# Branch A's tensor-engine order written out by hand, with the convolution taps kept out of the inverses

## The chip, the cores and the metric

The kernel runs on one core of a Trainium2 chip. The metric is the device time of one execution in microseconds (us), and the median of several runs stands for a kernel. The engines are named as the profile names them: PE is the tensor engine (PEld its weight load), DVE the vector engine, ACT the scalar engine, POOL the GpSimd engine, and SP the queue that issues nearly all DMAs.

## What is computed

The reference is a trunk of two layers over 256 context tokens and 512 latent tokens of 1024 channels, in float32. Each layer normalises and modulates its input, projects it with one wide matrix, runs four branches, and merges them through gates and an output matrix. Branch A is the one that matters here, with branch B's convolution beside it:

```python
def wkv_scan(s0, w, kk, b, k, v, r, reverse):
    def step(s, inp):
        w_t, kk_t, b_t, k_t, v_t = inp[:5]
        sa = jnp.einsum('bhvk,bhk->bhv', s, kk_t)
        s = s * w_t[:, :, None, :] - sa[..., None] * b_t[:, :, None, :] + v_t[..., None] * k_t[:, :, None, :]
        o = None if r is None else jnp.einsum('bhvk,bhk->bhv', s, inp[5])
        return s, o
...
def conv_module(glu, conv_w, conv_b, ln_w, ln_b):
    u = glu[..., :CONV_CH] * jax.nn.sigmoid(glu[..., CONV_CH:])
    u = lax.conv_general_dilated(u, conv_w[:, None, :], window_strides=(1,),
...
```

Branch A (8 heads of 64) runs `wkv_scan` forwards and backwards over context and latent tokens, normalises each head's output and adds a bonus. Branch B is a depthwise convolution of 31 taps over 512 channels. Branches C (windowed attention) and D (latent attention) follow in the kernel after branch A and are not touched by the change.

## The kernel before

Every large projection is a `dense`: 8 tiles of 128 input channels, each as three float32r matmuls (`mm3`: high by high, high by low, low by high), over 256 context columns and 512 latent columns. The weights of one output tile of 128 channels come by DMA (`raw`), ACT rounds them (`wh`) and POOL subtracts (`wl`), in two halves; three buffers of `wh` and `wl` are shared by all. The sums stand in the PSUM tag `d`, two banks, until ACT or DVE has taken them out.

Branch A works on four pairs of heads (p = 0 to 3). The sequence of 768 tokens is cut into 12 chunks of 64, taken two at a time (c = 0, 2, ... 10). For each pair:

- `rwkv_prep` makes decays and keys of 256 tokens at a time (three groups g), with short matmuls into the one bank of tag `E`.
- `rwkv_gram` makes the chunks' Gram matrices (`G`).
- `rwkv_inverse` inverts 32x32 blocks of all 12 chunks at once: ACT copies (L707), a DVE transpose (L710), 31 steps of two dependent DVE instructions (L717, L719), and two DVE transposes (L721, L722). PE takes no part in it.
- `rwkv_factors` turns the inverse into the factors `TM` with small PE matmuls (L739, L748).
- `rwkv_chunk` runs the recurrence. Each of the 12 chunks is three links: z (L820, then DVE makes `Xc`, L822), u (L826, then ACT copies one half, L827, and DVE the other, L828), q (L833, then DVE makes the new state `M`, L841). A link needs the one before.
- `rwkv_post` normalises the outputs and stores them.

`side_units` lists projections that branch A does not need: the convolution's gated input (`glu`, two tiles each, four of them), ten tiles for branches C and D, sixteen gates `z`, and three (layer 0) or eight (layer 1) tiles of branch gates. `fill` emits them in groups, FILL = 3, 3, 5, 7, 10, before and after the pairs, and what is left after the last pair. Each `glu` unit also emits its `conv_taps`: 31 DVE instructions (L966) on 256 context columns (layer 0 only) and 31 on 512 latent columns, with the lowest priority.

The order on each engine is fixed before the run. A planner, the tile scheduler, walks the program with a model of the instructions' times and takes on each engine the ready instruction of the highest priority (program order, shifted by `high_priority`). Where `manual_schedule` is set for PE, PE keeps the program's order instead; before the change that holds inside a few short groups of matmuls only. At run time each engine goes through its list in order and waits at semaphores.

Of the kernel before, what the change touches and what calls it, by code (L numbers as in the profile page):

```python
# [2 lines left out]

# [15 lines left out]
D = 1024  # L19
# [194 lines left out]

class Net:
# [70 lines left out]
    def mm3(self, ps, wh, wl, xh, xl, first, last):  # L286
        mm = self.nc.tensor.matmul
        mm(ps, lhsT=wh, rhs=xh, start=first, stop=False)  # L288
        mm(ps, lhsT=wh, rhs=xl, start=False, stop=False)  # L289
        mm(ps, lhsT=wl, rhs=xh, start=False, stop=last)  # L290

    def dense(self, w, xs, segs, psum=None):

        outs = []
        nk = len(xs)
        for s0, s1 in segs:
            ps = (psum or self.pd)(s1 - s0)
            outs.append(ps)
            for h, (wh, wl) in enumerate(w):
                for i in range(4):  # L300
                    k, c = 4 * h + i, slice(128 * i, 128 * i + 128)
                    self.mm3(ps, wh[:, c], wl[:, c], xs[k][0][:, s0:s1], xs[k][1][:, s0:s1], k == 0, k == nk - 1)
        return outs

    def proj(self, l, name, segs):

        if (name, segs) in self.begun:
            return self.begun.pop((name, segs))
        return self.dense(self.split_w(self.a["w_in"][l, TILES[name]]), self.hx, segs)
# [153 lines left out]
    def rwkv(self, l, rp):  # L463
# [35 lines left out]

        def fill(n):  # L500
            for _ in range(min(n, len(units))):
                units.pop(0)()

# [10 lines left out]
        for g in range(NG):  # L514
            self.rwkv_prep(rp, g, wa, st)
        self.rwkv_gram(rp, st)
        self.rwkv_factors(st, *self.rwkv_inverse(rp, st))
        self.rwkv_proj(l, rp, 1)
        fill(FILL[0])
        for p in range(4):  # L520
            nxt = None
            if p < 3:
                nxt = self.rwkv_state(l, rp, p + 1)
                self.rwkv_prep(rp, 0, wa, nxt)
            for c in (0, 2, 4, 6):
                self.rwkv_chunk(rp, st, c)
            if nxt:
                for g in range(1, NG):
                    self.rwkv_prep(rp, g, wa, nxt)
            self.rwkv_chunk(rp, st, 8)  # L530
            if nxt:
                self.rwkv_gram(rp, nxt)
                diag = self.rwkv_inverse(rp, nxt)
            self.rwkv_chunk(rp, st, 10)
            if nxt:
                self.rwkv_factors(nxt, *diag)
            if p == 2:
                right.close()
                self.window_inputs(l)
            self.rwkv_post(rp, p, st)  # L540
            if p == 3:
                self.window_rope()
            if p < 2:
                self.rwkv_proj(l, rp, p + 2)
            fill(FILL[p + 1])
            st = nxt
        fill(len(units))

    def rwkv_proj(self, l, rp, p, names="kvr", segs=(SEG_C, SEG_X)):

        nc = self.nc
        for nm in names:
# [3 lines left out]
            for ps, (s0, s1) in zip(self.proj(l, f"{nm}{p}", sg), sg):  # L556
# [7 lines left out]
    def rwkv_state(self, l, rp, p):  # L564
        nc = self.nc
        st = {"p": p, "KB": {}, "KR": {}, "v2": {}, "M": None, "o": {}, "c": None}
# [13 lines left out]
    def rwkv_prep(self, rp, g, wa, st):  # L580

# [35 lines left out]
        nc.tensor.matmul(ps, lhsT=self.c("blk"), rhs=sq, start=True, stop=True)  # L617
        kk = T("kk", "kk", 1)
# [4 lines left out]
        for d in range(2):  # L623
# [4 lines left out]
            ps = self.pE([128, n])  # L628
            lora(ps, 1, d)
            th = T("th", "th", 1)  # L630
            S.activation(th, ps, AF.Tanh, bias=dcol("a0h", dc), scale=0.5)
# [6 lines left out]
            ps = self.pE([128, n])  # L638
            lora(ps, 0, d)
            lw = T("lw")  # L640
            S.activation(rv(lw), ps, AF.Tanh, bias=dcol("w0h", dc), scale=0.5)
# [17 lines left out]
        if readout:  # L659
# [3 lines left out]
            nc.tensor.matmul(ps, lhsT=self.c("blk"), rhs=kds[0], start=True, stop=True)  # L663
            bv = T("bv")
# [3 lines left out]
    def rwkv_gram(self, rp, st):  # L668

        nc = self.nc  # L670
        mask = self.c("mask")
        st["G"] = []
        for c in range(0, NCH, 2):
            x, cl = c // GC, c % GC
            KB, KR = st["KB"][x], st["KR"][x]
            w = 64 if (self.last and x == 0) else 128
            G = rp.tile([128, 2, 2, 2, 128], F32, tag="G", name=self.n("G"), bufs=NCH // 2 + 1)
            st["G"].append(G)
            pss = [self.pA([128, 2, 2, 128]) for j in range(2)]
            for i in range(2):  # L680
                for d in range(2):
                    for j in range(2):
                        rows = slice(64 * j, 64 * j + 64)
                        nc.tensor.matmul(pss[j][:, i, d, :w],  # L684
                                         lhsT=KB[rows, d, cl + i].rearrange("p a b -> p (a b)"),
                                         rhs=KR[rows, cl + i, 0:w // 64, d, :],
                                         start=True, stop=True)
            for j, ps in enumerate(pss):
                nc.vector.tensor_tensor(out=G[:, j, :, :, :w].rearrange("p i d w -> p (i d) w"),  # L689
                                        in0=ps[:, :, :, :w].rearrange("p i d w -> p (i d) w"),  # L690
                                        in1=mask[:, :w].unsqueeze(1).to_broadcast([128, 4, w]), op=ALU.mult)

    def rwkv_inverse(self, rp, st):
# [16 lines left out]
        V.transpose(out=flat(B), in_=flat(AT))  # L710
# [11 lines left out]
        V.transpose(out=U.rearrange("p q t -> p t q"), in_=X.rearrange("p s t -> p t s"))  # L722
        return U, TA

    def rwkv_factors(self, st, U, TA):
# [7 lines left out]
        pss = []  # L733
        for q0, q1 in ((0, 16), (16, 24)):
# [6 lines left out]
            for d in range(2):  # L741
                b = slice(64 * d + 32, 64 * d + 64)
                S.copy(Y[b, q0:q1, :], ps[b])
            ps = self.pA([128, q1 - q0, 32])
# [15 lines left out]

    def rwkv_chunk(self, rp, st, c):
        cur = st["c"] or self.chunk_front(rp, st, c)
        st["c"] = self.chunk_front(rp, st, c + 2) if c + 2 < NCH else None
        self.chunk_back(rp, st, c, *cur)

    def chunk_front(self, rp, st, c):
# [20 lines left out]
        for d in range(2):  # L787
            h = half[1 - d]
            V.tensor_copy(VU[h, d], psb[h, 0])
        for i in range(2):  # L790
# [7 lines left out]
    def chunk_back(self, rp, st, c, KBt, VU, X0):  # L798

        nc, tc = self.nc, self.tc  # L800
# [3 lines left out]
        KR, G, TM, Dl = st["KR"][g], st["G"][c // 2], self.TM, st["Dl"]  # L804
        T = lambda nm, shape, bufs=2: rp.tile(shape, F32, tag=nm, name=self.n(nm), bufs=bufs)
        read = not (self.last and g == 0)
        Ms = []
        for i in range(2):
# [6 lines left out]
            u, q = (bank[:, x, 64:192].rearrange("p (a b) -> p a b", a=2) for x in range(2))  # L815
            X = X0[:, i]
            if M is not None:
# [4 lines left out]
                V.tensor_tensor(out=X, in0=X0[:, i], in1=z, op=ALU.subtract)  # L822
            for j in range(2):
                for d in range(2):
                    h = half[d]
                    mm(u[h, j], lhsT=TM[h, 2 * c + 2 * j + i, :], rhs=X[h, j], start=True, stop=True)  # L826
            S.copy(VU[half[0], 0, i], u[half[0]])  # L827
            V.tensor_copy(VU[half[1], 1, i], u[half[1]])  # L828
            if c + i == NCH - 1:
                break  # L830
            for d in range(2):
                for j in range(2):
                    mm(q[half[j], d], lhsT=KBt[:, i, d, j], rhs=VU[:, d, i, j], start=True, stop=True)  # L833
            st["M"] = M2 = T("M", [128, 2, 64], 3)
            if M is None:
                V.tensor_tensor(out=M2, in0=q, in1=D.to_broadcast([128, 2, 64]), op=ALU.mult)
                continue
            MD = T("MD", [128, 2, 64])
            nc.gpsimd.tensor_tensor(out=MD, in0=M, in1=D.to_broadcast([128, 2, 64]), op=ALU.mult)
            for d in range(2):  # L840
                V.scalar_tensor_tensor(out=M2[:, d], in0=q[:, d], scalar=D[:, d], in1=MD[:, d],  # L841
                                       op0=ALU.mult, op1=ALU.add)
        if not read:
            return
        po = self.pA([128, 2, 2, 64])
        with tc.manual_schedule(engines={mybir.EngineType.PE}):
            for i in range(2):
                m0 = Ms[i]
                for d in range(2):
                    for j in range(2):  # L850
                        mm(po[half[j], d, i], lhsT=VU[:, d, i, j], rhs=G[:, j, i, d, 64:128],
                           start=True, stop=m0 is None)
                    if m0 is not None:
                        for j in range(2):
                            mm(po[half[j], d, i], lhsT=m0[half[j], d], rhs=KR[half[j], cl + i, 1, d, :],
# [701 lines left out]
```

## Time and profile before

| | us |
|---|---|
| median of 3 runs (2697.1 to 2698.61) | 2698.14 |
| the profiled execution's own time | 2702.32 |
| span of the profiled execution, first to last instruction | 2700.2 |
| PE busy in the span | 2499.4 |
| DVE busy in the span | 1951.6 |
| ACT busy in the span | 1227.1 |
| POOL busy in the span | 607.5 |

The own time exceeds the span by 2.1 us. In the trace, layer 0's branch A lies between about 60 and 800 us and layer 1's between about 1570 and 2210 us. The four inverses of layer 0 run from 140 to 184, 287 to 345, 439 to 494 and 588 to 648 us; those of layer 1 from 1646 to 1709, 1798 to 1868, 1962 to 2006 and 2091 to 2132 us.

### The profile page before, as it was taken

What the parts mean: (1) busy time and instruction counts of PE and PEld (TensorE: products, weight loads), DVE (VectorE), ACT (ScalarE), POOL (GpSimd) and SP (SyncE); (2) the same over time, 40 slices, a digit from 0 to 9 for tenths busy, and PEclk for the clock granted to TensorE, in tenths of its full rate; (3) what the DMA queues carried; (4) which work ended last, traced back from release to release, by engine and by line L of the source; (5) the groups of instructions that cost most, each with busy time, mean ns of one, the idle gap of its engine ahead of it and who ended that gap; (6) DMA issues with size and microseconds to landing.
All of it is one profiled execution on the core that took longest, in us unless ns stands there. A gap on an engine that the chain in (4) does not pass through costs nothing. (4 is left out here: it accounts for less than half of the span.)

```text
span 2700.2 us, 48552 instructions
## 1 busy us (share of the span) xinstructions
PE 2499.4 (93%) x18622; PEld 1921.5 (71%) x18622; DVE 1951.6 (72%) x3836; ACT 1227.1 (45%) x2525; POOL 607.5 (22%) x644
## 2 busy tenths in 40 slices
PE   7999999898998998999999988897989889999998
PEld 5777778677785776776788877676666656666677
DVE  5898889888727664677633679989977757577835
ACT  5534454453325453445422453453555436555424
POOL 1232222122230111100132013323232231221140
PEclk9989989999899999999999999998999889999999
DMA  6321222213233346112222522323231322331333
GB/s 234 120 88 57 76 75 95 85 53 118 78 130 117 118 136 197 52 36 66 96 81 87 184 91 97 99 69 118 73 116 57 124 93 75 112 98 33 88 123 121
DMA packets 171031, 267.78 MB, mean 99 GB/s; under 512 B 18480, under 2 KB 69552, under 8 KB 170800
## 3 DMA queue, kind: packets, MB, share of 16 engines
q1 hardware_dynamic: 169520, 263.12, 30.6%
q8 instruction: 146, 2.39, 0.4%
q10 hardware_dynamic: 1280, 1.57, 0.2%
q14 instruction: 85, 0.70, 0.1%
HBM read 209.70 MB, written 54.92 MB: 98 GB/s over the span
## 5 line engine op out<-in xcount | busy, mean ns | idle before, releaser
L282 POOL TENSOR_TENSOR wl<-raw,wh 128x512 fp32r<-128x512 f32 x374 | 514.3, 1376 | 1547.7 <-ACT wh L281 1337.5
L288 PE MATMUL d<-hxh,wh 128*128 128x512 f32 (+1 forms) x1936 | 719.3, 372 | 26.8 <-DVE stg L923 11.6
L289 PE MATMUL d<-hxl,wh 128*128 128x512 f32 (+1 forms) x1936 | 717.4, 371 | 0.0
L290 PE MATMUL d<-hxh,wl 128*128 128x512 f32 (+1 forms) x1936 | 715.8, 370 | 0.0
L281 ACT CAST wh<-raw 128x512 fp32r<-128x512 f32 x420 | 259.5, 619 | 506.3 <-PE d L289 325.3
L288 PEld LDWEIGHTS d<-hxh,wh 128*128 128x128 f32 x1936 | 375.9, 194 | 82.4 <-DVE stg L931 12.0
L289 PEld LDWEIGHTS d<-hxl,wh 128*128 128x128 f32 x1936 | 376.3, 194 | 51.1 <-issue 2.0
L290 PEld LDWEIGHTS d<-hxh,wl 128*128 128x128 f32 x1936 | 375.8, 194 | 51.7 <-issue 1.6
L966 DVE SCALAR_TENSOR_TENSOR cacc<-cu,par,cacc 128x512 f32<-128x512 f32 (+1 forms) x360 | 280.9, 780 | 3.1
L288 PE MATMUL d<-uh,wh 128*128 128x512 f32 (+1 forms) x384 | 142.5, 373 | 9.9 <-ACT gt L1371 5.0
L1014 DVE TENSOR_REDUCE st<-S 128x1 f32<-128x768 f32 (+3 forms) x160 | 119.6, 763 | 33.7 <-PE S L1160 15.3
L289 PE MATMUL d<-ul,wh 128*128 128x512 f32 (+1 forms) x384 | 140.8, 368 | 0.2 <-DVE ul L1363 0.2
L290 PE MATMUL d<-uh,wl 128*128 128x512 f32 (+1 forms) x384 | 140.5, 366 | 0.0
L1378 DVE SCALAR_TENSOR_TENSOR gt<-gt,d 128x256 f32<-128x256 f32 (+1 forms) x72 | 42.8, 594 | 126.8 <-PE d L290 125.6
L719 DVE TENSOR_TENSOR X<-X,Xt 128x31 f32<-128x31 f32 (+15 forms) x248 | 111.1, 448 | 2.6
L717 DVE TENSOR_TENSOR Xt<-B,X 128x31 f32<-128x31 f32 (+15 forms) x248 | 101.4, 409 | 4.6 <-POOL X L712 1.7
L1020 ACT ACTIVATE mP<-S,st 128x768 f32<-128x768 f32 (+1 forms) x80 | 65.0, 814 | 68.7 <-DVE st L1016 64.1
L684 PE MATMUL A<-KR,KB 64*128 64x128 f32 (+1 forms) x768 | 80.0, 290 | 11.3 <-DVE KB L657 6.7
L288 PEld LDWEIGHTS d<-uh,wh 128*128 128x128 f32 x384 | 73.2, 192 | 23.8 <-ACT uh L1362 6.7
L707 ACT COPY AT<-G 32x128 f32<-32x128 f32 x192 | 79.3, 413 | 17.6 <-DVE G L689 15.3
L684 PEld LDWEIGHTS A<-KR,KB 64*128 64x128 f32 x768 | 67.2, 187 | 22.7 <-DVE KB L657 8.6
L289 PEld LDWEIGHTS d<-ul,wh 128*128 128x128 f32 x384 | 73.7, 192 | 11.0 <-DVE ul L1363 1.0
(325 smaller groups left out, 4781.6 us busy)
## 6 DMA issues: line engine op xcount, KB each, us to landing
raw<-in_w_in SPq DMA_DIRECT2D x316, 256.0 KB, 2.6
raw<-in_w_br SPq DMA_DIRECT2D x64, 256.0 KB, 2.7
ada<-in_ada_slim SPq DMA_DIRECT2D x64, 256.0 KB, 3.1
raw<-in_w_out SPq DMA_DIRECT2D x40, 256.0 KB, 2.7
ada<-in_ada SPq DMA_DIRECT2D x32, 256.0 KB, 5.4
spz<-stg SPq DMA_DIRECT2D x32, 256.0 KB, 2.9
kvx<-wa SPq DMA_DIRECT2D x24, 256.0 KB, 3.8
yl<-y SPq DMA_DIRECT2D x16, 384.0 KB, 3.6
```

The costliest lines, as they stand in the source:

```text
L281: nc.scalar.copy(hi, raw)
L282: self.low_engine.tensor_tensor(out=lo, in0=raw, in1=hi.bitcast(F32), op=ALU.subtract)
L288: mm(ps, lhsT=wh, rhs=xh, start=first, stop=False)
L289: mm(ps, lhsT=wh, rhs=xl, start=False, stop=False)
L290: mm(ps, lhsT=wl, rhs=xh, start=False, stop=last)
L684: nc.tensor.matmul(pss[j][:, i, d, :w], lhsT=KB[rows, d, cl + i].rearrange("p a b -> p (a b)"), rhs=KR[rows, cl + i, 0:w // 64, d, :], sta ...
L707: S.copy(AT[b, :, 4 * x:4 * x + 4].rearrange("p t q -> p q t"), G.rearrange("p j i d t -> p (j i) d t")[b, :, d, 32 * h:32 * h + 32])
L717: V.tensor_tensor(out=tv, in0=B[:, t, 0:t].unsqueeze(2).to_broadcast([128, t, w]), in1=X[:, t:t + 1, t:32].to_broadcast([128, t, w]), op=A ...
L719: V.tensor_tensor(out=X[:, 0:t, t:32], in0=X[:, 0:t, t:32], in1=tv, op=ALU.subtract)
L966: V.scalar_tensor_tensor(out=acc, in0=u[:, k:n + k], scalar=w, in1=acc, op0=ALU.mult, op1=ALU.add)
L1014: V.tensor_reduce(out=m[:, i:i + 1], in_=ps, axis=AX.X, op=ALU.max)
L1020: S.activation(P, ps.rearrange("p (k c) -> p k c", c=128), AF.Exp, bias=nm[:, i:i + 1], scale=scale, accum_out=tot[:, i:i + 1])
```

## The change

- **PE's order.** From the first chunk of pair 0 on, PE takes branch A in the written order. The chunk, prep, post and projection functions become generators that stop (`yield`) at each place where a dense run may lie. `pull(columns)` takes that many columns of matmuls from a queue (`flow`) of side units and of the projections of pair p + 2. After each link of the chain stands a run of `gap` columns, worked out at the start of each pair so that the queue ends with the last pair.
- **A reserve for each inverse.** Between the Gram matrices and the factors of the next pair lie 72,000 columns (WAIT): those of chunk 10's links and of two posts count, and the rest is pulled in one run.
- **Convolution taps.** They leave the `glu` units. The taps of convolution i may only start, on DVE, after the last transpose of inverse i, and an inverse's first transpose only after all taps emitted earlier. The taps on 512 columns are cut into two of 256.
- **Smaller parts.** The u sums of the two directions stand in two PSUM banks, not one; prep's two short projections share one `E` bank and one stop; prep's group 0, post's group 0 and the first Gram matrices are spread over the links of chunks 0 to 6; the first half of the next chunk's front is issued at a u link; the readout's matmuls are reordered; FILL is replaced by FIRST = 3 (three `glu` units before the pairs, as before) and the queue.

The diff, cut to its core:

```diff
+    def passes(self, ps, wh, wl, xh, xl, first, last):
...
+        yield n
         mm(ps, lhsT=wh, rhs=xh, start=first, stop=False)
...
+    def pull(self, columns):
+
+        self.debt += columns
+        while self.debt > 0 and self.flow:
+            n = next(self.flow[0], None)
+            if n is None:
+                self.flow.pop(0)
+            else:
+                self.debt -= n
+                self.left -= n
...
+        for steps, _ in units[:FIRST]:
+            drain(steps)
+        self.conv_taps(l, rp, 0, diag[-1])
+        for unit in units[FIRST:]:
+            self.queue(*unit)
+        with self.tc.manual_schedule(engines={mybir.EngineType.PE}):
+            st["front"] = drain(self.chunk_front(rp, st, 0))
+            for p in range(4):
+                st = self.rwkv_pair(l, rp, p, st, wa, right)
...
+        gap = max(GAP_MIN, (self.left - (3 - p) * (WAIT + SLACK)) // (32 * (3 - p) + 36))
+
+        for c in (0, 2, 4, 6):
+            for n, _ in enumerate(self.rwkv_chunk(rp, st, c)):
+                if small and n in (1, 4):
+                    next(small, None)
+                if nxt and c == 6 and n in (1, 4):
+                    self.rwkv_gram(rp, nxt, 2 * (n // 3))
+                self.pull(gap)
...
+        for _ in self.rwkv_chunk(rp, st, 8):
+            if small:
+                next(small, None)
+            self.pull(gap)
...
+            for c in range(4, NCH, 2):
+                self.rwkv_gram(rp, nxt, c)
+                self.pull(GRAM_GAP)
+            diag = self.rwkv_inverse(rp, nxt)
+            self.conv_taps(l, rp, p + 1, diag[-1])
+        before = self.left
+        for _ in self.rwkv_chunk(rp, st, 10):
+            self.pull(gap)
+        for _ in self.rwkv_post(rp, p, st, (1, 2)):
+            self.pull(POST_GAP)
...
+        if nxt:
+            self.pull(max(0, WAIT - (before - self.left)))
+            self.rwkv_factors(nxt, *diag)
+            self.pull(FACTOR_GAP)
...
+        first = V.transpose(out=flat(B), in_=flat(AT))
+        if self.last_tap is not None:
+            self.tc.add_manual_dep(first.ins, self.last_tap.name, mybir.DependencyInfo(
...
-            u, q = (bank[:, x, 64:192].rearrange("p (a b) -> p a b", a=2) for x in range(2))
+            u = [bank[half[d], d, 64:192].rearrange("p (a b) -> p a b", a=2) for d in range(2)]
+            q = bank[:, 1, 192:320].rearrange("p (a b) -> p a b", a=2)
...
-        with tc.high_priority(-1000000):
+        with tc.high_priority(-1000000), tc.issue_after(after):
...
+                    for x0 in range(0, n, TC):
...
+FIRST = 3
+
+GAP_MIN = 1536
+WAIT, SLACK = 72000, 9000
+GRAM_GAP, POST_GAP, FACTOR_GAP = 1024, 3072, 2048
```

## Rows read from the trace of the kernel before

**Rows 1.** The page, part 1: busy us, share of the span, instructions.
```profile
PE 2499.4 (93%) x18622; PEld 1921.5 (71%) x18622; DVE 1951.6 (72%) x3836; ACT 1227.1 (45%) x2525; POOL 607.5 (22%) x644
```

**Rows 2.** Layer 0: bounds, length, busy us (instructions) PE, PEld, DVE, ACT, POOL; granted clock.
```profile
140.50:185.00 44.50, 37.90 (x256) 32.46 (x255) 43.54 (x101) 6.91 (x13) 11.93 (x11) 0.92 0.27 83
185.00:648.00 463.00, 423.94 (x4057) 338.88 (x4057) 412.04 (x893) 213.16 (x465) 107.65 (x140) 0.95 0.25 78
185.00:286.90 101.90, 97.29 (x1026) 76.33 (x1026) 88.13 (x185) 57.20 (x130) 25.43 (x39) 0.92 0.22 68
648.00:735.00 87.00, 83.92 (x912) 62.05 (x911) 61.19 (x133) 36.26 (x74) 21.91 (x25) 0.86 0.29 91
735.00:800.00 65.00, 63.80 (x359) 55.99 (x360) 17.43 (x25) 15.94 (x30) 20.22 (x15) 1.00 0.35 115
```

**Rows 3.** Windows of layer 1, same columns.
```profile
1646.00:1710.00 64.00, 50.09 (x277) 41.66 (x277) 62.89 (x107) 14.34 (x26) 21.90 (x21) 0.90 0.30 102
1710.00:2132.00 422.00, 385.41 (x3560) 291.72 (x3557) 369.70 (x769) 207.84 (x446) 125.50 (x144) 0.96 0.28 91
2091.00:2132.00 41.00, 34.04 (x223) 26.23 (x223) 38.74 (x82) 16.62 (x26) 14.13 (x12) 0.94 0.37 125
2132.00:2205.00 73.00, 71.96 (x819) 49.65 (x814) 32.03 (x78) 30.05 (x62) 25.17 (x25) 0.92 0.31 100
```

**Rows 4.** Windows of the convolution taps alone (line 966): DVE busy.
```profile
140.50:185.00 44.50, 18.46 (x31) 0.92 0.27 83
185.00:648.00 463.00, 119.38 (x163) 0.95 0.25 78
648.00:800.00 152.00, 33.40 (x47) 0.92 0.31 101
1646.00:1710.00 64.00, 29.45 (x30) 0.90 0.30 102
1710.00:2132.00 422.00, 80.22 (x90) 0.96 0.28 91
```

**Rows 5.** Groups of instructions by line and shape: taps; busy, mean ns, idle before.
```profile
L966 DVE SCALAR_TENSOR_TENSOR cacc<-cu,par,cacc 128x512 f32<-128x512 f32 x240 | 209.6, 873 | 2.4
L966 DVE SCALAR_TENSOR_TENSOR cacc<-cu,par,cacc 128x256 f32<-128x256 f32 x120 | 71.3, 594 | 0.7
```

**Rows 6.** Waits of DVE, 185 to 648 us: total, times, longest.
```profile
DVE M L841 <- PE B L833: 11.3, 16, 2.5
DVE Xc L822 <- PE B L820: 6.6, 9, 3.1
DVE VU L828 <- ACT VU L827: 5.1, 12, 1.5
```

**Rows 7.** Timeline: two dense matmuls of one run, 24 starts apart.
```profile
143.13 0.40 PE L288 MATMUL d<-hxh,wh 128*128 128x512 f32 x1
...
148.60 0.28 PE L288 MATMUL d<-hxh,wh 128*128 128x256 f32 x1
```

**Rows 8.** Dense matmuls (first of each three) by shape, 648 to 735 us, then 2132 to 2205 us.
```profile
L288 PE MATMUL d<-hxh,wh 128*128 128x512 f32 x28 | 14.5, 517 | 0.0
...
L288 PE MATMUL d<-hxh,wh 128*128 128x256 f32 x32 | 9.7, 304 | 0.0
...
L288 PE MATMUL d<-hxh,wh 128*128 128x512 f32 x42 | 19.2, 458 | 0.0
```

**Rows 9.** Waits of PE, 185 to 648 us, then 1646 to 2132 us.
```profile
PE A L739 <- DVE TA L721: 17.9, 3, 9.1
PE d L288 <- DVE stg L931: 7.4, 4, 2.8
...
PE A L739 <- DVE TA L721: 33.3, 4, 13.8
```

**Rows 10.** Windows of 25 us: PE's busy share and the granted clock.
```profile
475.00:500.00 25.00, 15.91 (x227) 13.13 (x227) 22.45 (x51) 6.20 (x11) 4.26 (x5) 0.80 0.18 54
600.00:625.00 25.00, 20.73 (x113) 17.60 (x112) 25.00 (x48) 12.14 (x18) 7.06 (x4) 1.00 0.28 92
```

More of the change, by code (lines that the diff above doesn't have):

```diff
@@ L2 @@
 from contextlib import ExitStack
+from itertools import chain
 import numpy as np
@@ L211, in pack, with drain @@
     return {k: np.ascontiguousarray(v) for k, v in out.items()}
+def drain(steps):
+    while True:
+        try:
+            next(steps)
+        except StopIteration as e:
+            return e.value
 class Net:
@@ L301, in dense, with proj_steps, proj, queue @@
                     k, c = 4 * h + i, slice(128 * i, 128 * i + 128)
-                    self.mm3(ps, wh[:, c], wl[:, c], xs[k][0][:, s0:s1], xs[k][1][:, s0:s1], k == 0, k == nk - 1)
+                    yield from self.passes(ps, wh[:, c], wl[:, c], xs[k][0][:, s0:s1], xs[k][1][:, s0:s1], k == 0, k == nk - 1)
         return outs
-    def proj(self, l, name, segs):
+    def dense(self, *args):
+        return drain(self.dense_steps(*args))
+    def proj_steps(self, l, name, segs):
         if (name, segs) in self.begun:
             return self.begun.pop((name, segs))
-        return self.dense(self.split_w(self.a["w_in"][l, TILES[name]]), self.hx, segs)
+        return (yield from self.dense_steps(self.split_w(self.a["w_in"][l, TILES[name]]), self.hx, segs))
+    def proj(self, *args):
+        return drain(self.proj_steps(*args))
+    def pull(self, columns):
[7 more added lines that the diff above has]
+                self.left -= n
+        if not self.flow:
+            self.debt = 0
+    def queue(self, steps, columns, at=None):
+        self.flow.insert(len(self.flow) if at is None else at, steps)
+        self.left += columns
+    def finish(self, steps):
+        while any(x is steps for x in self.flow):
+            self.pull(512)
     def begin(self, l, pool):
@@ L498, in rwkv @@
         units = self.side_units(l, rp)
-        def fill(n):
-            for _ in range(min(n, len(units))):
-                units.pop(0)()
+        self.flow, self.debt, self.left, self.last_tap = [], 0, 0, None
         for segs in ((SEG_C,), (SEG_X,)):
@@ L626, in rwkv_prep @@
             dc = 4 * d + p
[L628 to L631, printed above, removed]
+            ps = self.pE([128, 2, n])
+            for x in range(2):
+                lora(ps[:, x], x, d)
+            yield
+            th, lw = T("th", "th", 1), T("lw")
+            S.activation(rv(lw), ps[:, 0], AF.Tanh, bias=dcol("w0h", dc), scale=0.5)
+            S.activation(th, ps[:, 1], AF.Tanh, bias=dcol("a0h", dc), scale=0.5)
             kd = T("kd", "kd", 2)
@@ L666, in rwkv_prep, with rwkv_gram @@
             nc.sync.dma_start(st["bon"][:, s0:s1], bv)
-    def rwkv_gram(self, rp, st):
+    def rwkv_gram(self, rp, st, c):
         nc = self.nc
         mask = self.c("mask")
[L672 to L691, printed above, removed]
@@ new lines, in rwkv_gram @@
+        x, cl = c // GC, c % GC
+        KB, KR = st["KB"][x], st["KR"][x]
+        w = 64 if (self.last and x == 0) else 128
+        G = rp.tile([128, 2, 2, 2, 128], F32, tag="G", name=self.n("G"), bufs=NCH // 2 + 1)
+        st["G"].append(G)
+        pss = [self.pA([128, 2, 2, 128]) for j in range(2)]
+        for i in range(2):
+            for d in range(2):
+                for j in range(2):
+                    rows = slice(64 * j, 64 * j + 64)
+                    nc.tensor.matmul(pss[j][:, i, d, :w],
+                                     lhsT=KB[rows, d, cl + i].rearrange("p a b -> p (a b)"),
+                                     rhs=KR[rows, cl + i, 0:w // 64, d, :],
+                                     start=True, stop=True)
@@ L693, in rwkv_inverse @@
+        for j, ps in enumerate(pss):
+            nc.vector.tensor_tensor(out=G[:, j, :, :, :w].rearrange("p i d w -> p (i d) w"),
+                                    in0=ps[:, :, :, :w].rearrange("p i d w -> p (i d) w"),
+                                    in1=mask[:, :w].unsqueeze(1).to_broadcast([128, 4, w]), op=ALU.mult)
     def rwkv_inverse(self, rp, st):
@@ L743, in rwkv_factors @@
                 S.copy(Y[b, q0:q1, :], ps[b])
+        self.pull(FACTOR_GAP)
+        pss = []
+        for q0, q1 in ranges:
             ps = self.pA([128, q1 - q0, 32])
@@ L789, in chunk_front @@
             V.tensor_copy(VU[h, d], psb[h, 0])
+        yield
         for i in range(2):
@@ L825, in chunk_back @@
                     h = half[d]
[L826 to L844, printed above, removed]
@@ L845, in chunk_back @@
-        po = self.pA([128, 2, 2, 64])
-        with tc.manual_schedule(engines={mybir.EngineType.PE}):
+                    mm(u[d][:, j], lhsT=TM[h, 2 * c + 2 * j + i, :], rhs=X[h, j], start=True, stop=True)
+            S.copy(VU[half[0], 0, i], u[0])
+            V.tensor_copy(VU[half[1], 1, i], u[1])
+            if i == 0 and c + 2 < NCH:
+                front = self.chunk_front(rp, st, c + 2)
+                next(front)
+            elif c + 2 < NCH:
+                st["front"] = drain(front)
@@ new lines, in rwkv_chunk @@
+            yield
+            if c + i < NCH - 1:
+                for d in range(2):
+                    for j in range(2):
+                        mm(q[half[j], d], lhsT=KBt[:, i, d, j], rhs=VU[:, d, i, j], start=True, stop=True)
+                st["M"] = M2 = T("M", [128, 2, 64], 3)
+                if M is None:
+                    V.tensor_tensor(out=M2, in0=q, in1=D.to_broadcast([128, 2, 64]), op=ALU.mult)
+                else:
+                    MD = T("MD", [128, 2, 64])
+                    nc.gpsimd.tensor_tensor(out=MD, in0=M, in1=D.to_broadcast([128, 2, 64]), op=ALU.mult)
+                    for d in range(2):
+                        V.scalar_tensor_tensor(out=M2[:, d], in0=q[:, d], scalar=D[:, d], in1=MD[:, d],
+                                               op0=ALU.mult, op1=ALU.add)
@@ L847, in chunk_back @@
+            if i == 0:
+                yield
+        if read:
+            po = self.pA([128, 2, 2, 64])
             for i in range(2):
-                m0 = Ms[i]
                 for d in range(2):
@@ L911, in plain @@
         def plain(name, segs):
-            for ps, (s0, s1) in zip(self.proj(l, name, segs), segs):
+            pss = yield from self.proj_steps(l, name, segs)
+            for ps, (s0, s1) in zip(pss, segs):
                 t = self.stage(rp, s1 - s0)
@@ L934, in mix @@
         def mix(b, f):
-            for ps, (s0, s1) in zip(self.proj(l, f"g{b}{f}", full), full):
+            pss = yield from self.proj_steps(l, f"g{b}{f}", full)
+            for ps, (s0, s1) in zip(pss, full):
                 t = self.stage(rp, s1 - s0)
```

198 lines of the change are left out of this document (110 added, 88 removed).

## The prediction

> **What bounds the kernel now.** The page's shares come first and mislead: PE reads 93% busy, DVE 72% [rows 1]. The second view, windows by stage, says where that is true. I cut branch A of each layer at the ends of its inverses. In layer 0 there are four kinds of stretch [rows 2]: the first inverse (44.5 us, DVE 43.54 busy); three periods of chain and inverse (463 us, DVE 412.04, 89%); the last pair's chain (87 us, DVE 61.19); and a tail of nothing but dense matmuls (65 us, PE 63.80, DVE 17.43). Layer 1 has the same first three [rows 3]: 64 us, 422 us (DVE 369.70, 88%) and 73 us (DVE 32.03), and no tail. So DVE, not PE, is nearly full while inverses and chains run, and PE alone is full where DVE has run out of work. The reader is to see two things that do not overlap: DVE's 412 us and PE's 65 us.
>
> The third view, the taps alone [rows 4], says what DVE does there: 18.46 us of taps lie in the first inverse of layer 0 and 29.45 us in that of layer 1. The last of the inverses of layer 1, which has no taps left, is 41 us long with 38.74 of DVE; the first, with them, is 64 [rows 3]. The fourth view, the waits, shows the price on PE: the factors wait for the inverse 17.9 us in three stops of layer 0 and 33.3 us in four of layer 1 [rows 9].
>
> The Trainium skill (Perfetto Trace Analysis, Identifying the Most-Contended Engine) warns that matmul busy share is no measure of PE's nearness to its limit, because matmuls are pipelined, and would have the weight loads' share read instead. The section 185 to 286.9 bears it out: PE 97.29 of 101.9, PEld 76.33 [rows 2]. By the first number PE could give back 4.6 us there, by the second up to 25.6; the sum below rests on neither.
>
> **The change, part by part.** All terms are differences to the profiled execution.
>
> *Dense columns.* A dense matmul of 512 columns starts every (148.60 - 143.13)/24 = 0.228 us [rows 7], 0.445 ns a column. From the diff, layer 0's queue holds 36,864 + 29 x 18,432 columns, and each of two projections adds 55,296. So gap is 2,906 columns (1.3 us) in pair 0 and about 3,500 (1.56 us) from pair 1 on; a middle pair takes 191,000 columns (85 us), the last 126,000 (56 us). Layer 1: 2,068, then about 2,600 columns; the last pair 93,700 (41.7 us). No matmul is added or saved.
>
> *The tail of layer 0.* The last pair's chain now has 84 x 512 + 96 x 256 = 67,600 dense columns [rows 8] (each counted three times), 30 us; the rest of its 87 us, 57, is short matmuls and waits. Afterwards 56 us of dense and this rest, of which I take 50 (between 44, what layer 1's last chain has, 73 - 28.7 [rows 3, 8], and 57): about 106 us in place of 87 + 65. That is 46 us less (bounds 39 and 52). What hides the moved dense work is the chain's waiting for DVE and ACT.
>
> *The first inverse.* Taps out: 43.54 - 18.46 = 25.1 us of DVE, and the 2.3 us that the inverse without taps loses (41 - 38.74) [rows 3, 4]: 44.5 becomes 27.4, -17. Layer 1: 62.89 - 29.45 + 2.3 = 35.7, in place of 64, -28. Dense work that PE did in those stretches goes between the links that follow, where PE is not what is late. If it is, some 10 us of each is lost again.
>
> *The three periods.* This is the part that speaks against the change: the taps are not removed, they move into the chain sections, where DVE is already 86% busy (88.13 of 101.9) [rows 2]. One convolution costs 171.2/4 = 42.8 us of DVE in layer 0, 109.7/4 = 27.4 in layer 1 [rows 4]. Three lie in the periods afterwards: 128.4 in place of 119.4 (+9), and 82.3 in place of 80.2 (+2). Cutting a 512-column tap in two costs between nothing (same elements) and 2 x 594 - 873 = 315 ns [rows 5]; both means hold waits for other engines, so I take the middle, 150 ns, x 93 taps = +14 us in each layer (bounds 0 and 29). Evacuations that move in from the tail: +4 in layer 0. DVE's work: 412 + 27 = 439, and 370 + 16 = 386.
>
> DVE's idle time is the unknown. Before it is 51.0 us in layer 0's three periods and 52.3 in layer 1's: 17 a period. Of it, waits for q, z and ACT's half of u are 11.3 + 6.6 + 5.1 us in layer 0 [rows 6], 7.7 a period. Chain instructions that stand in PE's order right after their run, and u in two banks, so that DVE's copy need not follow ACT's, can take away part of that; half is 3.8. The inverse without filler adds 2.3, and fixed runs sometimes too long for their link add something. Bounds: 6 us a period (nearly all chain waits gone) and 22 (none gone, 5 added); I take 14. Then layer 0's periods are 439 + 42 = 481 (+18) and layer 1's 386 + 42 = 428 (+6). PE needs 85 + 57 us and a little for prep and Gram of a layer 0 period of 160, so it is hidden.
>
> *Layer 1's last pair.* Dense 41.7 in place of 126 x 512 columns = 28.7 us [rows 8], rest 44 to about 40: +9 (bounds 4 and 13).
>
> *At nothing.* The u banks and the shared E bank (counted in the idle), the readout's order, spread prep, post and Gram steps: the same instructions in the sections' slack. Post's group 0 and its loads are earlier in SP's queue, next to weight loads that cover them. The taps take one load, two POOL clears and one store per segment along; POOL's clear of the second segment waits for the first segment's taps, and behind it on POOL stand the weights' subtractions, behind those PE's runs. Three buffers hold one and a half tiles, some 27,000 columns or eight runs, so it is covered unless POOL stands still for over 12 us.
>
> **Sum.** Layer 0: -17 + 18 - 46 = -45. Layer 1: -28 + 6 + 9 = -13. 2702.3 - 58 = 2644; the median of the runs lies 4 us below that execution, so 2640.
>
> **The rivals.**
>
> *Much faster.* The chain's waits all but vanish: idle at 6 a period (-48) and the cut taps free (-28): 2640 - 76 = 2564. For it: 23 us of link waits in layer 0 alone. Against: seven-eighths of all time in the periods is DVE work that stays.
>
> *Slower: taps in the links.* All 93 (layer 0) or 62 (layer 1) taps of a pair now lie beside its some 30 links outside the inverse, and DVE's order is fixed before the run. Where a tap stands ahead of a link's instruction that is ready, the chain waits, and PE, which may not slide dense work in any more, waits with it. One tap of 256 columns is 0.59 us [rows 5]. With 35 links in each of 8 pairs, 280 in all, the gain is gone at 58/280 = 0.21 us a link; at 0.3 us it ends at 2640 + 84 = 2724. Against it: taps had 0.87 us before and lay in the sections too (119 of 171 us fell in the periods), and half-size taps shorten the wait.
>
> *PE's clock.* A PE that waits in line might lose its clock: at 15.91 us of work in 25 it was granted 0.80, at 20.73 the full 1.00 [rows 10]. [...] I fold it into the slower rival.
>
> *No change.* The tail's 46 us are gained, but the periods grow by as much, with idle at 22 (+48) and the cut at 200 ns a tap (+9 for 186 taps): 2640 + 57 = 2697 against 2698.
>
> **How the numbers follow.** The forecast, DVE-bound periods with the tail absorbed, 2590 to 2690: 0.62. Much faster, below 2590: 0.13. No change, within 0.2% (5.4 us, about what a measurement here can tell from nothing): 0.05. Slower: 0.20. Faster in all 0.75. To leave out 2 in 10, the range cuts half of the much faster case and most of the slower one: 2585 to 2715.
>
> **What would show it.** Right: no stretch of pure dense work after layer 0's last chain; inverses of 28 to 44 us without a tap inside; PE's wait for the factors (L739) a few us in all; each section some 10 us longer than before in layer 0; DVE over 90% busy in the periods. Wrong: PE waits at L826, L833 or L820 growing to tens of us with taps just ahead on DVE (the slower rival); the factors late still, with 72,000 columns (32 us) used up before an inverse of 40; POOL standing at the clear of `cu` with PE waiting for weights; or sections no longer than before although all taps are in them (the much faster one).

## The result, and the profile after

The changed kernel takes 2799.11 us (median of 4 runs, 2793.9 to 2810.85) beside 2698.38 for the kernel before (4 runs): a ratio of 1.0379 with a 95% interval of 1.0346 to 1.0412. It is slower by 101 us, where I had forecast 58 us less and a range up to 2715. The profiled execution spans 2797.5 us, 97.3 more than before.

Page of the changed kernel, part 1, to be read against [rows 1]:

```profile
PE 2480.8 (89%) x18622; PEld 1914.3 (68%) x18622; DVE 2015.3 (72%) x4084; ACT 1231.5 (44%) x2525; POOL 635.0 (23%) x644
```

The same matmuls, PE's share down from 93% to 89%. The windows of the changed kernel, with the columns of [rows 2], cut at the ends of the inverses: first inverse, three periods and last pair of layer 0, then of layer 1.

```profile
141.00:176.00 35.00, 27.91 (x219) 24.64 (x219) 32.83 (x68) 5.50 (x10) 8.05 (x7) 0.94 0.20 61
176.00:718.00 542.00, 458.56 (x4264) 371.95 (x4260) 456.30 (x1014) 228.80 (x488) 121.56 (x153) 0.91 0.24 76
718.00:841.00 123.00, 113.74 (x1189) 90.08 (x1187) 89.45 (x193) 45.26 (x90) 35.45 (x34) 0.97 0.34 106
1683.00:1720.00 37.00, 27.26 (x179) 22.21 (x179) 34.84 (x69) 6.58 (x11) 12.52 (x10) 0.90 0.29 91
1720.00:2198.00 478.00, 389.39 (x3640) 295.41 (x3636) 386.74 (x871) 208.38 (x449) 136.03 (x148) 0.90 0.25 78
2198.00:2306.00 108.00, 91.05 (x842) 65.49 (x841) 68.16 (x145) 39.08 (x78) 47.46 (x34) 0.91 0.34 109
```

The reader is to see the second and fifth lines. In the periods neither engine is full: DVE is idle for 542 - 456.30 = 85.7 us and 478 - 386.74 = 91.3 us, PE for 83.4 and 88.6. Before, DVE was idle for 51.0 and 52.3 us there [rows 2, 3].

Whose idle time makes the kernel longer is read from the sums over branch A of both layers (length, then PE, PEld, DVE, ACT, POOL). First the kernel before, from 140.5 to 801 and 1646 to 2211 us:

```profile
sum 1225.50, PE 1120.15 PEld 874.32 DVE 1003.78 ACT 527.17 POOL 335.54; mean PE 560.07 PEld 437.16 DVE 501.89 ACT 263.59 POOL 167.77
```

Then the changed kernel, the six windows above together:

```profile
sum 1323.00, PE 1107.91 PEld 869.78 DVE 1068.32 ACT 533.60 POOL 361.07; mean PE 184.65 PEld 144.96 DVE 178.05 ACT 88.93 POOL 60.18
```

Branch A is 97.5 us longer, which is all of the span's growth. PE's work is 12 us less, and its idle time goes from 105.4 to 215.1 us. So the loss is PE standing still. What it waits for, over the whole span of the changed kernel (total, times, longest):

```profile
PE E L758 <- DVE kd L756: 85.0, 18, 7.6
PE A L890 <- DVE VU L884: 39.4, 8, 6.6
PE B L938 <- DVE VU L928: 16.1, 15, 5.4
...
PE B L919 <- DVE M L946: 12.0, 14, 1.8
...
PE A L836 <- DVE TA L818: 11.7, 3, 5.3
```

And the two rows of the kernel before that answer to the first and the last of these:

```profile
PE A L739 <- DVE TA L721: 53.3, 8, 13.8
...
PE E L663 <- DVE kd L661: 3.6, 4, 1.2
```

The wait for the inverse shrank from 53.3 to 11.7 us, as it was meant to. But the matmul of prep that makes the bonus (L663, now L758) went from 3.6 us of waiting for DVE (and 2.5 for ACT) to 85.0, and the second half of a chunk's front (L890) stands for 39.4 us, where the answering row before (L794) is 1.2 us. Neither is a link of the chain. The timeline of the changed kernel (start, duration, instruction) shows one such stop:

```profile
303.97 1.64 DVE L739 TENSOR_TENSOR_SCAN L<-cst,lw 128x256 f32<-128x256 f32 x1
305.53 0.39 DVE L733 TENSOR_TENSOR kd<-kd,kvx 128x256 f32<-128x256 f32 x1
...
306.64 0.41 DVE L750 TENSOR_TENSOR KR<-r,E 128x256 f32<-128x256 f32 x1
306.98 0.41 DVE L751 TENSOR_TENSOR KB<-kd,lw 128x256 f32<-128x256 f32 x1
307.32 0.41 DVE L752 SCALAR_TENSOR_TENSOR KB<-th,lw 128x256 f32<-128x256 f32 x1
307.65 0.41 DVE L755 TENSOR_TENSOR kd<-kd,kd 128x256 f32<-128x256 f32 x1
308.10 0.48 DVE L756 SCALAR_TENSOR_TENSOR kd<-r,par,kd 128x256 f32<-128x256 f32 x1
308.73 0.76 PE L758 MATMUL E<-kd,cst 128*128 128x256 f32 x1 [6.12 <-DVE kd L756]
```

The bonus matmul is issued one stop of the generator after prep's short projections. DVE needs a string of scans and products to make `kd` for it; there is no tap among them (over all 18 stops at L758, DVE spends 0.6 us on taps). PE reaches L758 with that string still running and stands 6.12 us, with tens of thousands of dense columns in the queue behind it that may not pass.

### The profile page after: what moved, and what is told of

It reads as the page before. It is cut to its first block, busy times and chain, and to the rows that moved or that the text cites. A ratio compares the mean times of both kernels' runs of the same rounds, so it can differ in the third digit from the quotient of the medians.

```text
span 2797.5 us, 48786 instructions
## 1 busy us (share of the span) xinstructions
PE 2480.8 (89%) x18622; PEld 1914.3 (68%) x18622; DVE 2015.3 (72%) x4084; ACT 1231.5 (44%) x2525; POOL 635.0 (23%) x644
## 5 line engine op out<-in xcount | busy, mean ns | idle before, releaser
L292 POOL TENSOR_TENSOR wl<-raw,wh 128x512 fp32r<-128x512 f32 x374 | 524.6, 1404 | 1624.2 <-ACT wh L291 1351.2
L305 PE MATMUL d<-hxh,wl 128*128 128x512 f32 (+1 forms) x1936 | 725.0, 375 | 4.3 <-POOL wl L292 4.2
L1086 DVE SCALAR_TENSOR_TENSOR cacc<-cu,par,cacc 128x256 f32<-128x256 f32 x600 | 316.9, 568 | 4.7
L758 PE MATMUL E<-kd,cst 128*128 128x256 f32 x40 | 20.4, 607 | 85.0 <-DVE kd L756 85.0
L944 POOL TENSOR_TENSOR MD<-M,Dl 128x128 f32<-128x128 f32 x80 | 45.0, 562 | 188.5 <-DVE M L946 160.6
```

The source lines that it names most:

```text
L292: self.low_engine.tensor_tensor(out=lo, in0=raw, in1=hi.bitcast(F32), op=ALU.subtract)
L1086: t = V.scalar_tensor_tensor(out=acc[:, x0:x1], in0=u[:, x0 + k:x1 + k], scalar=w, in1=acc[:, x0:x1], op0=ALU.mult, op1=ALU.add)
```

## The experiments

Three theories. **Theory 1:** PE's written order puts matmuls that are not links ahead of what makes their operands, and each stop is paid in full. **Theory 2:** the loss is DVE's: taps moved into the sections, and cut. **Theory 3:** the runs between the links are too long and lie on the chain's own path. All ratios are to the kernel before on the same chip, with 95% intervals; its medians there lie between 2698.9 and 2702.9 us, so a difference in us between two runs of different groups is uncertain by some 4 us.

**The bonus matmul later.** In `rwkv_prep`, three stops more ahead of the bonus:

```diff
+            for _ in range(BONUS_LATER):
+                yield
+BONUS_LATER = 3
```

> The changed kernel with three more stops ahead of the bonus matmul of each prep group, so that it stands three runs later in PE's order; nothing else. Theory 1 (stops in line): PE's written order puts this matmul one link after the last short projection, while DVE still has some 5 to 8 us of the group's work before it; PE stands 41.8 us at it in layer 0 and 39.9 us in layer 1, and dense work cannot pass. Then these stops fall to under 25 us in all and the time falls by 50 to 80 us, to 2720 to 2750. Theory 2 (DVE and the taps): the sections are as long as DVE's work, which the moved and cut taps raised; then PE stands at the next matmul instead (Gram, chunk 10) and the time stays within 15 us of 2799.

Measured: 2757.78 us, 1.0212 (1.0173 to 1.0252), 41 us less than the changed kernel. Its waits of PE:

```profile
PE A L892 <- DVE VU L886: 39.1, 8, 7.2
PE E L760 <- DVE kd L756: 28.3, 10, 7.1
PE B L940 <- DVE VU L930: 22.6, 20, 3.2
PE d L305 <- POOL wl L292: 17.2, 2, 14.9
```

The stop fell by 57 us and the time by 41; the front's stop stayed. This is the direction of theory 1, by less than it said: waits at the links rose (L938's 16.1 us in the changed kernel to 22.6 at the same matmul, here L940), and in this execution one subtraction on POOL lasted 16.61 us, where the median is 1.29, and held PE up for 14.9.

**The front later too.** The second half of the next pair's first front goes behind the reserve. Its operand is a DVE copy (L884). In the changed kernel that copy stands in line among the inverse's steps and post's instructions at six of the eight stops; at pair 0's two, with 7.7 of the 39.4 us, taps stand ahead of it.

```diff
-            nxt["front"] = drain(self.chunk_front(rp, nxt, 0))
+            front = self.chunk_front(rp, nxt, 0)
+            next(front)
...
+            nxt["front"] = drain(front)
```

> The same, and the second half of the next pair's first front stands after the inverse's reserve, not before it. PE stands 39.4 us at that place in the changed kernel (8 stops), since DVE's two copies are queued among the inverse's steps. Theory 1: another 20 to 35 us less than the first kernel, 2690 to 2725, near the kernel before. Theory 2: within 15 us of 2799.

Measured: 2728.04 us, 1.0096 (1.0069 to 1.0124), another 30 us. The front's row fell to 7.7 us and left the longest:

```profile
PE E L762 <- DVE kd L758: 27.7, 10, 7.1
...
PE A L894 <- DVE VU L888: 7.7, 2, 5.9
```

Moving the two matmuls later gave back 71 of the 101 us.

**The order without the taps' edits.** The written order stays; taps are emitted in `glu`, whole and free, as before.

```diff
+        self.conv_taps(l, rp, i)
...
-                    for x0 in range(0, n, TC):
+                    for x0 in range(0, n, n):
```

> The changed kernel with the taps as before: emitted with their glu unit, on 512 columns at once, free to lie in the inverses. Theory 1: the stops in line remain, and inverses stretched again by 15 to 25 us of taps outlast the 72,000 columns of reserve; 2780 to 2840. Theory 2: without the moved taps the time is back at the kernel before or below it, 2650 to 2710.

Measured: 2838.04 us, 1.0499 (1.0473 to 1.0525), 39 us slower than the changed kernel. Its waits of PE:

```profile
PE E L756 <- DVE kd L754: 101.5, 18, 10.1
PE A L834 <- DVE TA L816: 35.0, 4, 21.6
PE A L888 <- DVE VU L882: 33.9, 8, 6.6
```

Taps inside an inverse make it outlast the reserve (one stop of 21.6 us). So with PE's order fixed, the taps' edits together are a gain; theory 2 has the sign wrong for this kernel.

**The taps' edits without the order.** The kernel before, with taps tied behind the inverses and cut, the planner ordering PE:

```diff
-        with tc.high_priority(-1000000):
+        with tc.high_priority(-1000000), tc.issue_after(after):
...
+                    for x0 in range(0, n, TC):
```

> The kernel before with the taps alone changed: tied behind each inverse and cut to 256 columns, PE's order left to the planner. Theory 1: the planner slides dense work into the waits, so the shorter inverses and the longer sections about balance; 2670 to 2720. Theory 2: the sections grow by the taps' work, some 10 us a pair, and nothing returns it; 2740 to 2800.

Measured: 2748.17 us, 1.0164 (1.0118 to 1.0209), in theory 2's range. Its longest wait of PE is still the factors':

```profile
PE A L747 <- DVE TA L729: 40.7, 8, 8.3
```

It fell from 53.3 to 40.7 us, and the kernel lost 45 (against 2702.89 for the kernel before on the same chip). Where the planner orders PE, the taps' edits cost time by themselves. The next runs part them.

**Whole taps in the changed kernel.**

```diff
-                    for x0 in range(0, n, TC):
+                    for x0 in range(0, n, n):
```

> The changed kernel with the 512-column taps whole again, nothing else. In the runs so far DVE spent 345 us on 620 taps where they are cut and 266 us on 372 where they are not, so the cut costs some 79 us of DVE. If DVE's work sets the sections (theory 2), nearly all of it comes back: 2725 to 2755. If PE's stops in line set them (theory 1), DVE's lighter queue shortens those stops only where a tap stood in it, and the time is 2775 to 2799.

Measured: 2794.46 us, 1.0349 (1.0322 to 1.0375). Five us less, which the intervals do not part from the changed kernel. The cut cost less than the expectation says: DVE's busy time fell by 31.4 us (from 2015.3 to 1983.9), not by 79, for the 266 us came from a run whose taps lie elsewhere. Of these 31.4 us five show in the time, and by the intervals at most some 20, so the cut is at most a small part of the 101.

**Both mends with whole taps.** The two edits before that, together with whole taps.

> The later bonus matmul and front (2728 us) with whole taps. Theory 2: 70 us less, 2650 to 2680, faster than the kernel before. Theory 1: with the two largest stops mended already, 2700 to 2728. Both may hold in part: then 2680 to 2705.

Measured: 2719.2 us, 1.007 (1.0043 to 1.0096), 9 us less than with cut taps, though the two intervals overlap a little. That is in theory 1's range. The bonus still stops PE for 28.6 us.

**Taps behind the inverses, whole, the planner's order.** As the run with the taps' edits alone, without the cut.

> The kernel before with whole taps tied behind each inverse, PE's order left to the planner (with cut taps it took 2748 us). If the cut was what made that slower, 2680 to 2710; if the place of the taps did, 2735 to 2750.

Measured: 2714.32 us, 1.0055 (1.0032 to 1.0077). So of the 45 us lost there, the place of the taps makes 15 and the cut some 30; the time lies between the two expectations. In the planner's order the cut's 30.3 us of DVE work (2022.8 against 1992.5) show in the time; in the written one five did. What the place costs does not read as waiting: PE's busy time is 2521.8 us here and 2499.4 in the kernel before [rows 1], its idle time no longer. Why is not shown.

**Short runs.** As the run with both mends and whole taps, with `gap` fixed:

```diff
-        gap = max(GAP_MIN, (self.left - (3 - p) * (WAIT + SLACK)) // (32 * (3 - p) + 36))
+        gap = 1024
```

> The later bonus matmul and front with whole taps, and runs of 1,024 columns in place of some 2,900 and 3,500 (layer 0) and 2,100 and 2,600 (layer 1) after each link; the rest of the queue is left for after the last pair, where nothing lies beside it. Theory 3 (a run between two links lies on the chain's own path and costs its full length): the steps get shorter by what the tail gets longer, and the time stays within 15 us of the kernel with whole taps. If the runs are hidden by the links' waits instead, the steps keep their length and the tail comes on top, 60 us and more.

Measured: 2807.31 us, 1.0401 (1.037 to 1.0432), 88 us worse than with the long runs. Windows of this kernel, the end of layer 0's branch A:

```profile
770.00:848.00 78.00, 78.00 (x451) 69.03 (x450) 7.34 (x13) 20.06 (x38) 24.80 (x20) 1.00 0.33 108
```

The dense work that was not placed comes back as a tail, 78 us of PE alone with DVE at 7.34, and what the links gained did not pay for it. How much they gained is read from PE's link matmuls (the three lines that write the tile `B`), from the first to the last of a layer: 80.5 us less in layer 0 (574.8 to 494.3) and 30.5 us less in layer 1 (518.6 to 488.1), 111 in all. What follows the last links is 199 us longer. Its waits of PE:

```profile
PE E L762 <- DVE kd L758: 49.8, 14, 8.2
PE B L942 <- DVE VU L932: 28.9, 26, 3.6
PE B L923 <- DVE M L950: 28.7, 32, 2.9
```

With both mends and long runs these were 28.6, 21.5 and 11.5 us. So neither expectation holds in full. Of the runs taken out, some 111 of 199 us had lain on the chain's own path, as theory 3 says, and the other 88 had cost nothing: they covered the waits of the links, and the bonus's too. Shorter runs alone are no mend, but a run after each link is not free either.

**The planner's order, everything else as changed.** The one statement that fixes PE's order goes; emission order, reserve, taps and banks stay.

```diff
-        with self.tc.manual_schedule(engines={mybir.EngineType.PE}):
+        with ExitStack():
```

> The changed kernel without the one statement that holds PE to the written order: the same program, taps, runs and banks, but the planner lays out PE as it does elsewhere. Theory 1 (the written order makes PE stand in line): the stops at the bonus matmul (81.7 us) and at the front (39.4 us) shrink to under 40 us together, and the time falls to 2690 to 2740. Theory 2 (the moved and cut taps fill DVE): the sections stay as long, 2770 to 2800. A third outcome, if the planner takes dense work ahead of the chain: above 2800 with few stops.

Measured: 2706.55 us, 1.0026 (1.0012 to 1.0041), in theory 1's range. This one line gives back 93 of the 101 us. Its waits of PE:

```profile
PE A L836 <- DVE TA L818: 37.5, 8, 8.9
PE E L758 <- DVE kd L756: 14.0, 15, 1.7
...
PE A L890 <- DVE VU L884: 8.0, 5, 4.7
```

And its sums over branch A (same columns as above):

```profile
sum 1231.00, PE 1123.95 PEld 879.10 DVE 1067.97 ACT 532.12 POOL 355.61; mean PE 561.98 PEld 439.55 DVE 533.99 ACT 266.06 POOL 177.81
```

DVE does the same 1068 us of work as in the changed kernel; PE's idle time is back at 1231 - 1124 = 107 us. The bonus and the front stop PE for 22.0 us in place of 124.4. The factors' wait is up again, to 37.5 us: what the written order gains at the inverses is a quarter of what it pays at the two stops.

**The order, mended further.** Both mends, whole taps, BONUS_LATER = 6, pair 0's front ahead of the region with the written order, and both halves of u copied by ACT:

```diff
-            V.tensor_copy(VU[half[1], 1, i], u[1])
+            S.copy(VU[half[1], 1, i], u[1])
```

> The written order with whole taps, the front behind the reserve (2719 us), and three more mends: the bonus matmul six runs later, pair 0's first front left to the planner ahead of the glu units, and both copies of u on ACT, since DVE's copy waits for ACT's in every kernel so far (52.1 us of DVE idle in the changed kernel, in spite of the two banks). Theory 1: the stops left at the bonus (28.6 us), at u's copy (21.5) and at pair 0's front (6 a layer) go: 2670 to 2700. If other stops take their place as fast as these go, 2705 to 2725.

Measured: 2678.46 us, 0.9921 (0.99 to 0.9943). It is some 20 us under the kernel before, with the written order. The three new mends were not run apart. What is left on PE at the links and the bonus:

```profile
PE B L923 <- DVE M L950: 17.1, 18, 2.5
PE B L930 <- DVE Xc L925: 15.4, 18, 1.9
PE E L762 <- DVE kd L758: 13.3, 6, 3.9
```

**ACT's copies alone, in the kernel before.**

> The kernel before with both copies of u on ACT, nothing else. If DVE's wait for ACT's copy (20.1 us idle) and its own 0.29 us are on the chain there, 20 to 30 us less, 2670 to 2682; if the planner's dense work fills them, within 8 us of 2699.

Measured: 2690.5 us, 0.9969 (0.9951 to 0.9986), 8 us less, at the edge of the second outcome: less than half of the 20.1 us of wait shows in the time.

**The mended kernel in the planner's order.** As the mended one, without the statement that fixes PE's order.

> The mended kernel (2678 us) without the statement that holds PE to the written order. If the written order, once its stops are mended, is worth something in itself (dense work held back for the inverses), the planner's order is slower, 2685 to 2710. If the mends and the ACT copies alone make the gain, the planner does at least as well, 2655 to 2680.

Measured: 2640.88 us (five runs: three at 2640.7 to 2640.9, the others 2653.09 and 2656.67), 0.9806 (0.978 to 0.9832), the fastest of all and below the range of the second outcome. That is 60 us under the kernel before by the medians, and 45 to 59 by the interval. Its page, part 1, its waits of PE, and its sums over branch A:

```profile
PE 2456.4 (93%) x18622; PEld 1897.1 (72%) x18622; DVE 1952.9 (74%) x3740; ACT 1255.1 (48%) x2621; POOL 634.2 (24%) x644
```

```profile
PE A L840 <- DVE TA L822: 19.5, 5, 5.3
...
PE E L762 <- DVE kd L758: 10.4, 8, 2.9
...
PE B L930 <- DVE Xc L925: 7.2, 10, 1.7
...
PE B L923 <- DVE M L950: 4.4, 8, 1.4
```

```profile
sum 1175.00, PE 1089.00 PEld 855.74 DVE 1008.66 ACT 558.73 POOL 360.75; mean PE 544.50 PEld 427.87 DVE 504.33 ACT 279.37 POOL 180.38
```

Even mended, the written order costs 2678.46 - 2640.88 = 38 us by the medians, and 31 by the two ratios, whose intervals lie apart. With it, z and u (L923, L930) wait 32.5 us; without it, 11.6. From the first link to the last, the two layers together take 1064 us with it and 1028 without.

## Why the prediction was wrong, point by point

**The step that failed** is DVE's idle time in the periods: "I take 14" us a period, within bounds of 6 and 22, and PE "is hidden". Measured were 85.7/3 = 28.6 and 91.3/3 = 30.4 us. That DVE would be over 90% busy in the periods was my sign of being right; it was 84 and 81%, and PE, no more hidden than DVE, stood idle about as long. I compared each engine's sum of work with the period's length and took the larger. That holds where one engine can slide work into the other's waits. In a written order PE cannot: its stops and DVE's waits follow one another and add. I priced only waits that stood in the trace of before (links and factors), and had the spread prep, post and Gram steps "at nothing", as "the same instructions in the sections' slack". In the trace of before the planner had put dense work and the running pair's own matmuls ahead of the bonus matmul (3.6 us of waiting for DVE); of that cover a run of some 1.3 us and at most one link were left at two of the three prep groups (their stops last 5.5 to 7.6 us, those of the first group 1.5 to 2.1), and the price was 85.0 us, with 39.4 more at the front. Two later placements gave back 71 us, and freeing the order 93. Nor were the runs after the links hidden in full: over half of what the short runs took out had lain on the chain's path.

**The sum.** The excesses over my terms: first inverses 35.0 and 37.0 us against 27.4 and 35.7 (+8.9), periods 542 and 478 against 481 and 428 (+111, of which DVE's idle time is 93 and its work 18), last pairs 123 and 108 against 106 and 88 (+37; 88 is the 79 us from 2132 to 2211 before, and 9). That makes 157, and 2644 + 157 = 2801 beside 2799.3 for the profiled execution. The last pairs' 37 us are another term that was mis-sized: their two windows hold 161,792 and 115,200 dense columns where I had 126,000 and 93,700. That is 57,000 more, some 25 us at 0.445 ns a column; PE's idle time there is 26 us in all, the largest row 7.4. In layer 0's first inverse I took the taps' busy time off DVE's and had 25.1 us; it reads 32.83 without them.

**Right: taps, cut, tail, clock.** No tap lies in any of the eight inverses. In the periods taps take 141.36 us in layer 0 and 91.95 in layer 1, where I had 128.4 + 14 and 82.3 + 14. Over the kernel the cut added 36.0 us to 240 taps, 150 ns each, the value taken. That was luck: I had only two bounds, 0 and 315 ns, and took the middle.

```profile
L1086 DVE SCALAR_TENSOR_TENSOR cacc<-cu,par,cacc 128x256 f32<-128x256 f32 x600 | 316.9, 568 | 4.7
```

That is 316.9 against 209.6 + 71.3 [rows 5]. DVE's work in layer 1's periods came out at 386.74 where I had 386, in part by luck, with 4 us less of taps and as much more elsewhere; layer 0's is 456.30 against 439: taps and evacuations (4.4 us more) as said, the rest in many groups, the scans of prep first (12.9 to 15.5 us). The stretch of dense work alone at the end of layer 0 is gone: the last link ends at 823 us and the branch at 841. The granted clock fell from 0.95 to 0.91 in layer 0's periods [rows 2], and from 0.96 to 0.90 in layer 1's [rows 3]; between the two levels of 1.2 and 2.4 GHz that is a little more time at the lower level, and over branch A PE's busy time did not grow (1120.15 to 1107.91 us). POOL's weights held PE's runs up for 4.2 us in all.

**Wrong: the u banks.** I had DVE's copy of u free of ACT's. It waits longer than before. Who DVE's u copy waited for (us, times), in the kernel before and then in the changed one:

```profile
  ACT VU L827: 20.1, 33
```

```profile
  ACT VU L927: 52.1, 30
```

In both traces DVE's copy waits for a semaphore that ACT's copy raises, in two banks as in one; why the program carries it is not shown. The Trainium skill (PSUM — Partial Sum Buffer, Specifications (TRN2)) has ScalarE and VectorE access PSUM in parallel as long as they do not collide on a bank. No run here shows these two copies doing so.

**The slower rival** had the sign and not the cause. It put the loss at taps ahead of ready links, with waits at L820, L826 and L833 of tens of us. The answering rows are 12.0, 9.2 and 16.1 us. Taps are part of them: laid over the trace, DVE is at a tap for 20.6 of the 41.8 us that PE stands at these three lines, whatever the row names. That is 0.15 us a link over 280 links, with or without a tap, where the rival needed 0.21, and most of PE's 215.1 us of idle time lies at stops with no tap ahead. Whole taps took only five us off the time, and letting the taps loose made it worse (2838.04).

**Open.** Why the mended written order still loses 31 to 38 us is shown by place (the chain from first to last link) and not by cause; the runs that lie on the chain's path are a candidate. Which of the edits make the 60 us of the fastest kernel was not separated: ACT's copies alone gave 8, and the planner's order with cut taps and no mends was 8 us slower than the kernel before. Whether the second u bank is worth anything without the semaphore was not tried.

## What to carry to other kernels

Before an engine's order is written out, list every instruction that will stand in it, not only the chain's links: for each, what makes its operand, how long that takes, and whether the work written ahead of it covers that; the waits in a trace made by a planner show none of these prices, since it had covered them. Take a window's length less each engine's busy time as the test of who binds: where no engine was full, as here, sums of work did not forecast the length, and stops in line added. Emission order and reserves may be worth keeping while the planner keeps the last word: here the same edits gave 2678 us with a fixed order and 2641 without.

## What the runs showed that I had not expected

PE's busy time is not a fixed quantity: the same 18,622 matmuls took 2499.4 us before [rows 1] and 2456.4 in the fastest kernel, at mean granted clocks of 0.962 and 0.963. So 43 of the 61 us between the two profiled executions came out of time that had read as PE at work.

What a tap costs DVE depends on where it lies, and a cut is priced only against whole taps in the same place. Against whole taps that may lie in the inverses (the order without the taps' edits) the cut reads as (316.9 - 259.7)/240 = 238 ns:

```profile
L1085 DVE SCALAR_TENSOR_TENSOR cacc<-cu,par,cacc 128x512 f32<-128x512 f32 x240 | 193.2, 805 | 2.7
L1085 DVE SCALAR_TENSOR_TENSOR cacc<-cu,par,cacc 128x256 f32<-128x256 f32 x120 | 66.5, 554 | 1.2
```

In the run that differs from the changed kernel by the cut alone, they read:

```profile
L1086 DVE SCALAR_TENSOR_TENSOR cacc<-cu,par,cacc 128x512 f32<-128x512 f32 x240 | 210.2, 876 | 4.5
L1086 DVE SCALAR_TENSOR_TENSOR cacc<-cu,par,cacc 128x256 f32<-128x256 f32 x120 | 70.6, 588 | 3.8
```

That is (316.9 - 280.8)/240 = 150 ns. The whole tap went from 873 [rows 5] to 805 ns and back to 876 with nothing changed in it.
